# Weight splits, combinations and the norm's root in the first chunks of two MLP stages

## The chip, the cores and the metric

The kernel runs on one core of a Trainium2 chip. The metric is device time in microseconds (us) of the whole program, as the median of several runs. The core has engines that each work through a queue of their own in order: TensorE (PE in the profile, with its weight loads as PEld), VectorE (DVE), ScalarE (ACT), GpSimd (POOL) and SyncE (SP), which here issues the transfers. An instruction that waits holds up all that stands behind it in its queue.

## The reference

The program computes a trunk of two layers for 768 tokens (a sequence of 512 and one of 256) of width 1024. Layer 0 mixes tokens by windowed attention, layer 1 by a short gated convolution. Behind each mixer come the MLP and a gated embedding. The MLP, where the change lies, is the two lines in the middle:

```python
def rms_norm(x, g):
    y = x * lax.rsqrt(jnp.mean(x * x, axis=-1, keepdims=True) + EPS)
    return y * g
...
for i in range(DEPTH):
    h = rms_norm(x, norm_mix[i])
    x = x + mixer(h)
    h = rms_norm(x, norm_mlp[i])
    x = x + jnp.square(jax.nn.relu(h @ mlp_w_up[i])) @ mlp_w_down[i]
    gate = jax.nn.sigmoid(rms_norm(x, norm_ple[i]) @ ple_w_gate[i])
    x = x + (p[i] @ ple_w_proj[i]) * gate
return rms_norm(x, final_norm)
```

All is in float32. `mlp_w_up` is 1024 x 4096, `mlp_w_down` 4096 x 1024.

## The kernel before, in words

**Float32 from three products.** Every operand of a matmul is split into a rounded high part (a copy by ACT) and a low part (the difference, by DVE), and a product is high x high + high x low + low x high. So each weight tile costs a copy on ACT (`high`, line 409) and a subtraction on DVE (`low`, line 420) before PE can use it. `zhi` and `zlo`, `whi` and `wlo`, `vhi` and `vlo` are such pairs; the tag `z` has one buffer, `w` two.

**Tiling of the MLP.** The 4096 hidden features are cut into 16 chunks of 256 (`u` = 0 to 15), two chunks make a group `g`, and after each group come two `down` jobs (`h` = 0, 1), which add the group's part to `x`. Tokens lie along the free axis in two halves of 384. A *plain* chunk (`up_plain`) multiplies its two 128-feature weight tiles with both token halves straight: four results `p1`, `p2` (two banks each), 24 matmuls for each bank. The other chunks (`up`) and all `down` jobs use a scheme with seven products for a 2 x 2 block instead of eight (`product7`), which needs sums of weight blocks (`sums32`, `sums14`) and *combinations* of activation blocks: `norm.combine(m)` makes, for each of four pairs of blocks of `x`, two scaled copies `q` on ACT, four half-width steps on DVE (`t13`, `t42`), two high copies on ACT and two low parts on DVE. `PLAIN = 3, 2` says that chunks 0, 1, 2 are plain in the first MLP (`mlp0`) and chunks 0, 1 in the second (`mlp1`): the time they take on PE is used to make the combinations. In `mlp1` two of the four combinations are made ahead of it (`early = 2`), in `mlp0` none.

**The norm.** The gain is multiplied into `x` when its blocks are split (`Norm7.block`), and the factor 1/root is applied to the chunk's result (`rectified`, line 863). For it the squares of all blocks are added up in `acc`; `acc_parts` splits the sum (`ah`, `al`), `sum_squares` adds over partitions by four matmuls with ones (`ss`), and `rstd_steps` gives three steps: `logs` (an ACT table load, `v` on DVE, `ln` twice and `y` = exp on ACT), `newton` (a square on ACT, `v` on DVE) and `result` (`rstd` on DVE).

**Order.** Inside `mlp` the order on PE, ACT and DVE is the order of the program's text (`manual_schedule`); what stands ahead of it, the mixer's output projection with its adds, squares and block splits, is ordered by a scheduler and may be mixed with the first instructions of `mlp`. The list `pend` holds the steps that make a finished chunk's activations ready for `down`; `late()` takes one of them, `weave` takes one step from each of several lists in turn.

`up_plain` issues its matmuls in four parts, n = 0 to 3, and after each part the work of the other engines. For chunk 0 the parts are: blocks 0 to 5 into `p1`, the same into `p2`, blocks 6 and 7 into `p1`, and into `p2`. For later chunks they are one bank each: `p1` and `p2` of the second token half, then `p1` and `p2` of the first. Behind part 0 stand the next chunk's fetch (`make`) and the split of its `second` weight tile (`whi`, `wlo`), woven with a combination; behind part 1 another combination and `pend`; behind part 2 the split of the next chunk's `direct` tile (`zhi`, `zlo`), which waits until PE has read the old one for the last time; behind part 3, in chunk 0, the root with a third combination. Then `rectified` empties the banks and `squared` follows. The next chunk's first matmul reads `zhi`, its third `zlo`.

In the listing, lines 170 to 261 are the norm, 879 to 950 `up_plain`, 952 to 1005 `up`, 1079 to 1092 the list of jobs. In the trace `mlp0` starts at 310.4 us with chunk 0, 1 at 327.8, 2 at 352.8; `mlp1` at 1144.0 with chunk 0, 1 at 1161.5, 2 at 1178.3.

Of the kernel before, what the change touches and what calls it, by code (L numbers as in the profile page):

```python
# [18 lines left out]
P = 128  # L19
D = 1024  # L20
KB = D // P
# [14 lines left out]
NG = FF // (FG * P)  # L36

H = T // 2
# [3 lines left out]
EXP_LN = "natural_log_exp_and_others"  # L42
# [5 lines left out]
def trunk_kernel(ctx: ExitStack, tc: tile.TileContext, a: dict, out: bass.AP):  # L48
# [56 lines left out]
    def bank(tag, name):  # L105
        return psum.tile([P, 512], F32, tag=tag, name=name, bufs=BANKS[tag])
# [9 lines left out]
    def both(name="mm", tag=None):  # L116

        return [t[:, :H] for t in fresh(name, 2, tag)]
# [52 lines left out]
    class Norm:  # L171
# [30 lines left out]

        aside = temp

        def acc_parts(self):
            ah, al = self.aside("ah", F32R), self.aside("al", F32R)
            self.last = split(ah, al, self.acc)
            return ah, al

        def sum_squares(self, psum, also=None, parts=None, tag=None):  # L210

# [22 lines left out]
        def rstd_steps(self, psum, ss=None):  # L234
            n = self.n
            if ss is None:
                ss = self.sum_squares(psum)
            v, ln, y = (self.aside(name) for name in ("v", "ln", "y"))

            def logs():  # L240
                with tc.issue_after(self.last):
                    act.preload_act_table_set(EXP_LN)
                for t, o, e in ss:
                    dve.tensor_scalar(v[:, o:e], t, 1.0 / D, EPS, ALU.mult, ALU.add)  # L244
                for t, o, e in ss:
                    act.activation(ln[:, o:e], t, AF.Ln, scale=1.0 / D, bias=eps[:])  # L246
                act.activation(y, ln, AF.Exp, scale=-0.5)  # L247


            def newton():  # L250
                act.activation(ln, y, AF.Square)  # L251
                dve.scalar_tensor_tensor(v, ln, -0.5, v, ALU.mult, ALU.mult)  # L252

            def result():
                if self.rplace is None:
                    self.r = stat.tile([P, n], F32, tag="rstd", name=f"rstd_{self.name}")[:]
                else:
                    self.r = slot(self.rplace, f"rstd_{self.name}", F32)[:, :n]
                dve.scalar_tensor_tensor(self.r, v, 1.5, y, ALU.add, ALU.mult)  # L259

            return [logs, newton, result]
# [184 lines left out]
    def mixer_attention():  # L446
# [36 lines left out]
                yield ps[:, :n], o, o + n  # L483
                o += n

        def step(i, w, part, tag, vector):

            l, m = i // KB, i % KB
            if tag == "L":
                t = ap.tile([P, T], F32, tag="L", name="pjs", bufs=BL)  # L490
            else:
                t = big("pjs")
            for ps, o, e in products(terms_of(w, part, col=m % 4 * P)):
                if vector:
                    dve.tensor_copy(t[:, o:e], ps)
                else:
                    act.activation(t[:, o:e], ps, AF.Copy)
            nc.sync.dma_start(pj[l][m], t[:])

        with tc.manual_schedule(engines=order):  # L500
# [31 lines left out]
            w0 = blocks(hi[:], 2), blocks(lo[:], 2)  # L532
            w1 = weight(None, 2, raw=w1)
            for i in range(KB):
                step(i, (w0, w1)[i // 4], part0, "L", i % 2)
# [13 lines left out]
        with s1:  # L549
# [208 lines left out]

            def projected(q):
                w = weight(a["proj"][1, q], 2)  # L760
                for i in range(4):
                    step(KB + 4 * q + i, w, part1, "t", False)

            part1 = [], []

# [87 lines left out]
    def mlp(l, norm, nxt, w, places, early):  # L853
# [11 lines left out]
        def squared(t):  # L865
            act.activation(t[:], t[:], AF.Square)  # L866
# [24 lines left out]
        def late(n=1):  # L891

            for _ in range(n):
                if pend:
                    pend.pop(0)()

        def up_plain(u, w, make, then):

            nonlocal r

            ps = [both(f"p{i + 1}", {0: "AA", 1: "BC"}.get(u, "AA")[i]) for i in range(2)]
            y1 = y2 = None

            def rects(*which):
                for i, o in which:
                    rectified((y1, y2)[i], ps[i][o], H * o, H * o + H, ALU.max)


            order = [(0, (0, 6), (0, 1)), (1, (0, 6), (0, 1)), (0, (6, 8), (0, 1)), (1, (6, 8), (0, 1))]
            if u > 0:  # L910
                order = [(i, (0, 8), (o,)) for o in (1, 0) for i in range(2)]
            for n, (i, ks, sides) in enumerate(order):
                for k in range(*ks):
                    m, h = PAIRED[k] % (KB // 2), PAIRED[k] // (KB // 2)
                    c = slice(P * m, P * m + P)
                    hi, lo = w.w[f"w{i + 1}{h + 1}"]
                    for j, (wt, part) in enumerate(((hi, 0), (hi, 1), (lo, 0))):
                        for o in sides:
                            pe.matmul(
                                ps[i][o],  # L920
                                lhsT=wt[:, c],
                                rhs=xs[f"x{h + 1}{1 + o}"][m][part],
                                start=k == 0 and j == 0,
                                stop=k == KB - 1 and j == 2,
                            )
                if n == 0:
                    v = make()
                    split2 = [lambda: v.split("second")] if v.plain else []
                    todo1 = norm.combine(todo.pop(0)) if todo else []
                    rest, pend[:] = pend[:4], pend[4:]  # L930
                    weave(rest, todo1, split2)
                elif n == 1:
                    if r is None:
                        parts = norm.acc_parts()
                    sums = [] if v.plain else [v.sums32, v.sums14, lambda: v.split("direct")]
                    weave(norm.combine(todo.pop(0)) if todo else [], sums, pend)
                    pend.clear()
                elif n == 2:
                    v.split("direct" if v.plain else "s32")
                    if u > 0:  # L940
                        y1, y2 = big("y1"), big("y2")
                        rects((0, 1), (1, 1))
                else:
                    if r is None:
                        steps = norm.rstd_steps(psum, norm.sum_squares(psum, parts=parts, tag="C"))
                        weave(steps, norm.combine(todo.pop(0)) if len(todo) > 1 else [])
                        r = norm.r
                        y1, y2 = big("y1"), big("y2")
                        rects((0, 1), (1, 1))
                    rects((0, 0))  # L950
                    squared(y1)
                    rects((1, 0))
                    pend.extend(acts_of(u, y1, y2, y2))
            return v

        def up(u, w, make, then):

            w.low("s32")
            w.split("s14")
            late()  # L960
            v = make()
            seven = isinstance(v, Weights7)
            a = bank("A", "a")[:, :H]
            product7(a, w, "w11", xs, True)
            late()
            c = bank("C", "c")[:, :H]
            act.activation(c, a, AF.Copy)  # L967
            late()
            w.split("w22")
            late()  # L970
            b = bank("B", "b")[:, :H]
            product7(b, w, "s3", xs, True)
            p = big("p")[:, :H]
            act.activation(p, b, AF.Copy)
# [101 lines left out]
                        add(m, ps[i])  # L1076
                        nxt.block(m, x(m))

        jobs = [(up_plain, 0), (up_plain, 1)]
        for g in range(NG - 1):  # L1080
            jobs += [(up if 2 * g + 2 >= PLAIN[l] else up_plain, 2 * g + 2), (down, g, 0), (down, g, 1), (up, 2 * g + 3)]
# [159 lines left out]

    n1 = Norm7(2, "mlp0", xs0, act0[7:11], act0[11])
    w0, behind = first_chunk(0, n1, 0)
    w = [weight(a["w_o0"][2], 4), weight(a["w_o2"], 2)]
    for i, m in enumerate(PAIRED):
        if i == 4:
            w[0] = weight(a["w_o0"][3], 4)
        ps = both()
        if m < KB // 2:
            group2(ps, terms_of(w[0], [p[4:] for p in aos], col=m % 2 * P))  # L1250
        else:
            group2(ps, terms_of(w[1], [p[6:] for p in aos], col=(m - 4) * P))
        add(m, ps, xa[m])
        n1.block(m, x(m))
        behind(i)
# [96 lines left out]
```

## Time and profile before

| | us |
|---|---|
| median of 3 runs | 1716.2 |
| lowest and highest | 1715.09, 1717.12 |
| the profiled execution | 1715.87 |
| its span, first to last instruction | 1714.1 |
| PE busy | 1672.0 |
| DVE busy | 1339.6 |
| ACT busy | 855.7 |

Rows of a timeline read: start in us, busy us, engine, line of the kernel, operation, output<-input, partitions x elements, how many in a row; in brackets the idle time just ahead and what ended it. Starts of instructions that follow each other closely lie nearer than their busy times, since the engines overlap the end of one with the start of the next. Rows of waits read: engine, what waited, for whom, us in total, how often, the longest. Rows of windows read: stretch, its length, then busy time of PE, PEld, DVE, ACT and POOL with the number of instructions, the clock granted to PE as a share of full, the share of DMA engines busy, and GB/s.

### The profile page before, as it was taken

The numbers are of one execution on the slowest core, as the hardware profiler recorded it, in microseconds if no ns is written. First come the engines' busy times: TensorE is split into PE (matmuls) and PEld (weight loads), VectorE is DVE, ScalarE is ACT, GpSimd is POOL, SyncE is SP. The second block draws the span as 40 slices with busy tenths as digits, with TensorE's granted clock in tenths as the row PEclk, the third lists the DMA queues.
The fourth block names the chain that finished last, engine by engine and source line by source line (L and its number), as shares of the span: only waits on it lengthen the run. The fifth ranks groups of instructions, "written<-read, shape, count | busy, mean of one in ns | idle before, by whom it ended". The sixth has DMA issues, their size and how long they took to land. (4 is left out here: it accounts for less than half of the span.)

```text
span 1714.1 us, 24208 instructions
## 1 busy us (share of the span) xinstructions
PE 1672.0 (98%) x9554; PEld 1616.8 (94%) x9554; DVE 1339.6 (78%) x2198; ACT 855.7 (50%) x1363; POOL 2.0 (0%) x30
## 2 busy tenths in 40 slices
PE   8999999979999999999999999999999999999996
PEld 7887878979999999999999999999999999999986
DVE  7587788878999999977764444667989999999676
ACT  6467756645455455545541111445455555545454
POOL 0000000000000000000000000000000000000000
PEclk9999999989999999999999999999999999999998
DMA  8653331112221222122312121211221222222222
GB/s 263 189 146 110 114 109 62 45 50 74 65 84 62 75 74 74 62 84 93 108 62 62 62 62 62 76 60 49 74 73 64 74 75 74 65 71 86 74 89 96
DMA packets 47554, 143.80 MB, mean 84 GB/s; under 512 B 6048, under 2 KB 10656, under 8 KB 47440
## 3 DMA queue, kind: packets, MB, share of 16 engines
q1 hardware_dynamic: 44880, 139.10, 25.8%
q10 hardware_dynamic: 2560, 3.15, 0.7%
q8 instruction: 75, 1.23, 0.3%
q14 instruction: 39, 0.32, 0.1%
HBM read 122.31 MB, written 10.48 MB: 77 GB/s over the span
## 5 line engine op out<-in xcount | busy, mean ns | idle before, releaser
L83 ACT ACTIVATE whi<-wraw 128x1024 fp32r<-128x1024 f32 (+2 forms) x74 | 76.6, 1035 | 183.9 <-PE b L129 53.2
L409 ACT ACTIVATE whi<-sum 128x1024 fp32r<-128x1024 f32 x55 | 57.9, 1053 | 146.6 <-PE a L441 146.6
L866 ACT ACTIVATE y<-y 128x768 f32<-128x768 f32 x64 | 53.4, 838 | 140.5 <-DVE y L863 140.5
L84 DVE TENSOR_TENSOR wlo<-wraw,whi 128x1024 fp32r<-128x1024 f32 (+2 forms) x74 | 88.2, 1191 | 11.7 <-ACT whi L83 11.4
L441 PE MATMUL a<-act,whi 128*128 128x384 f32 x448 | 96.7, 337 | 0.0
L441 PE MATMUL a<-t,zhi 128*128 128x384 f32 x440 | 90.7, 337 | 1.8 <-ACT c L967 1.8
L441 PE MATMUL b<-t,zhi 128*128 128x384 f32 x440 | 90.5, 337 | 0.9 <-DVE y L863 0.9
L441 PE MATMUL a<-t,whi 128*128 128x384 f32 x440 | 90.5, 337 | 0.0
L1023 DVE TENSOR_TENSOR x<-x,a 128x384 f32<-128x384 f32 x112 | 60.8, 553 | 35.1 <-PE a L441 34.8
L441 PE MATMUL a<-xs,whi 128*128 128x384 f32 x432 | 84.5, 337 | 0.0
L138 PE MATMUL mm<-xs_mix,whi 128*128 128x512 f32 (+1 forms) x320 | 83.3, 342 | 0.0
L441 PEld LDWEIGHTS a<-t,zhi 128*128 128x128 f32 x440 | 77.9, 188 | 2.1 <-ACT c L967 2.1
L441 PEld LDWEIGHTS a<-act,whi 128*128 128x128 f32 x448 | 79.8, 188 | 0.0
L441 PEld LDWEIGHTS b<-t,zhi 128*128 128x128 f32 x440 | 77.7, 188 | 1.2 <-issue 1.2
L441 PEld LDWEIGHTS a<-t,whi 128*128 128x128 f32 x440 | 77.8, 188 | 0.0
L441 PEld LDWEIGHTS a<-xs,whi 128*128 128x128 f32 x432 | 76.3, 188 | 0.0
L420 DVE TENSOR_TENSOR wlo<-wraw,whi 128x1024 fp32r<-128x1024 f32 x60 | 73.0, 1217 | 1.9 <-ACT whi L409 1.9
L420 DVE TENSOR_TENSOR wlo<-sum,whi 128x1024 fp32r<-128x1024 f32 x55 | 67.2, 1222 | 9.2 <-ACT whi L409 9.2
L409 ACT ACTIVATE whi<-wraw 128x1024 fp32r<-128x1024 f32 x60 | 63.2, 1054 | 17.4 <-issue 10.3
L420 DVE TENSOR_TENSOR zlo<-sum,zhi 128x1024 fp32r<-128x1024 f32 x55 | 66.9, 1217 | 1.9 <-ACT zhi L409 1.9
L409 ACT ACTIVATE zhi<-sum 128x1024 fp32r<-128x1024 f32 x55 | 58.3, 1060 | 19.9 <-DVE sum L385 16.1
L330 ACT ACTIVATE t<-y 128x768 fp32r<-128x768 f32 x56 | 47.0, 841 | 40.6 <-DVE y L321 27.9
(279 smaller groups left out, 4647.9 us busy)
## 6 DMA issues: line engine op xcount, KB each, us to landing
wraw<-in_up SPq DMA_DIRECT2D x64, 512.0 KB, 3.5
wraw<-in_down SPq DMA_DIRECT2D x64, 512.0 KB, 3.5
wraw<-in_w_in SPq DMA_DIRECT2D x24, 512.0 KB, 3.4
wraw<-in_gate SPq DMA_DIRECT2D x16, 512.0 KB, 3.5
pj<-pjs SPq DMA_DIRECT2D x16, 384.0 KB, 2.9
wraw<-in_w_q SPq DMA_DIRECT2D x8, 512.0 KB, 4.9
wraw<-in_w_out SPq DMA_DIRECT2D x8, 512.0 KB, 3.4
x_in<-in_x SPq DMA_DIRECT2D x8, 384.0 KB, 7.2
```

Source lines behind the costliest of these rows:

```text
L83: first = act.activation(hi, src, AF.Copy)
L84: dve.tensor_tensor(lo, src, hi.bitcast(F32), ALU.subtract)
L138: pe.matmul(ps[:, o:e], lhsT=w, rhs=x[:, o:e], start=i == 0 and j == 0, stop=i == n - 1 and j == 2,)
L330: act.activation(t[0][:], (self.q1, self.q2)[i][:], AF.Copy)
L409: act.activation(hi[:], src, AF.Copy)
L420: dve.tensor_tensor(lo[:], src, hi[:].bitcast(F32), ALU.subtract)
L441: pe.matmul(ps, lhsT=a, rhs=b, start=start and i == 0, stop=i == len(terms) - 1, skip_group_check=True)
L866: act.activation(t[:], t[:], AF.Square)
L1023: dve.tensor_tensor(t[:, o : o + H], t[:, o : o + H], f, op)
```

## The change

The table load leaves `logs` for a method of its own, which loads once:

```diff
+        ready = False
+        def table(self):
+            if not self.ready:
+                with tc.issue_after(self.last):
+                    act.preload_act_table_set(EXP_LN)
+            self.ready = True
...
             def logs():
-                with tc.issue_after(self.last):
-                    act.preload_act_table_set(EXP_LN)
+                self.table()
```

In `up_plain`, chunk 0 (`not known`) splits the sum of squares and loads the table behind part 0, ahead of the combination; adds over partitions behind part 0 where `early` is set (`mlp1`) and behind part 1 otherwise; and takes the root behind part 1, with one combination between `logs` and `newton`. The split of the next chunk's direct tile stays behind part 2 in chunk 0, and moves ahead of part 1's combination in later chunks. Only two combinations are left in chunk 0 of `mlp0`.

```diff
+            known = r is not None
...
                 if n == 0:
                     v = make()
                     split2 = [lambda: v.split("second")] if v.plain else []
-                    todo1 = norm.combine(todo.pop(0)) if todo else []
                     rest, pend[:] = pend[:4], pend[4:]
-                    weave(rest, todo1, split2)
+                    if not known:
+                        parts = norm.acc_parts()
+                        norm.table()
+                    weave(rest, norm.combine(todo.pop(0)) if todo else [], split2)
+                    if not known and early:
+                        ss = norm.sum_squares(psum, parts=parts, tag="C")
                 elif n == 1:
-                    if r is None:
-                        parts = norm.acc_parts()
+                    if not known and not early:
+                        ss = norm.sum_squares(psum, parts=parts, tag="C")
+                    steps = [] if known else norm.rstd_steps(psum, ss)
+                    for step in steps[:1]:
+                        step()
+                    if known and v.plain:
+                        v.split("direct")
                     sums = [] if v.plain else [v.sums32, v.sums14, lambda: v.split("direct")]
                     weave(norm.combine(todo.pop(0)) if todo else [], sums, pend)
                     pend.clear()
+                    for step in steps[1:]:
+                        step()
+                    r = norm.r
                 elif n == 2:
-                    v.split("direct" if v.plain else "s32")
-                    if u > 0:
+                    if not v.plain:
+                        v.split("s32")
+                    elif not known:
+                        v.split("direct")
+                    if known:
                         y1, y2 = big("y1"), big("y2")
                         rects((0, 1), (1, 1))
                 else:
-                    if r is None:
-                        steps = norm.rstd_steps(psum, norm.sum_squares(psum, parts=parts, tag="C"))
-                        weave(steps, norm.combine(todo.pop(0)) if len(todo) > 1 else [])
-                        r = norm.r
+                    if not known:
                         y1, y2 = big("y1"), big("y2")
-                        rects((0, 1), (1, 1))
+                        rects((0, 1))
                     rects((0, 0))
                     squared(y1)
+                    if not known:
+                        rects((1, 1))
                     rects((1, 0))
```

In `up`, the first chunk behind the plain ones of `mlp1` (`first`) takes its results `c` and `b` from bank tag A instead of C and B, and takes its first three `late` steps behind the copy into `c`:

```diff
+            first = u == PLAIN[l] <= 2
...
-            late()
+            if not first:
+                late()
...
-            late()
-            c = bank("C", "c")[:, :H]
+            if not first:
+                late()
+            c = bank("A" if first else "C", "c")[:, :H]
             act.activation(c, a, AF.Copy)
-            late()
+            late(3 if first else 1)
...
-            b = bank("B", "b")[:, :H]
+            b = bank("A" if first else "B", "b")[:, :H]
```

The places of the activations in `mlp0` are taken in another order; the second combination gets 14, 0, 1 and 2 instead of 14, 16, 17 and 18 (16 to 19 hold the attention's output before, 0 to 6 a copy of `x`):

```diff
-    xs0 = [*range(32, 42), *range(8, 15), *range(16, 20), *range(7)]
+    xs0 = [*range(32, 42), *range(8, 15), *range(7), *range(16, 20)]
```

The rest (how `step`, the list of jobs and the weights of the last output projection are written) leaves the instructions and their order as they were. The number of matmuls, copies and subtractions is the same; PE's queue differs only in the place of the eight `ss` matmuls.

More of the change, by code (lines that the diff above doesn't have):

```diff
@@ L484, in products, with step @@
                 o += n
-        def step(i, w, part, tag, vector):
-            l, m = i // KB, i % KB
+        def step(l, m, w, part, tag, vector):
             if tag == "L":
@@ L534, in mixer_attention @@
             for i in range(KB):
-                step(i, (w0, w1)[i // 4], part0, "L", i % 2)
+                step(0, i, (w0, w1)[i // 4], part0, "L", i % 2)
                 norm.block(i, xin(i))
@@ L760, in projected @@
                 w = weight(a["proj"][1, q], 2)
-                for i in range(4):
-                    step(KB + 4 * q + i, w, part1, "t", False)
+                for m in range(4 * q, 4 * q + 4):
+                    step(1, m, w, part1, "t", False)
             part1 = [], []
@@ L1077, in last_down @@
                         nxt.block(m, x(m))
-        jobs = [(up_plain, 0), (up_plain, 1)]
+        ups = [(up if u >= PLAIN[l] else up_plain, u) for u in range(2 * NG)]
+        jobs = ups[:2]
         for g in range(NG - 1):
-            jobs += [(up if 2 * g + 2 >= PLAIN[l] else up_plain, 2 * g + 2), (down, g, 0), (down, g, 1), (up, 2 * g + 3)]
+            jobs += [ups[2 * g + 2], (down, g, 0), (down, g, 1), ups[2 * g + 3]]
         with tc.manual_schedule(engines={ET.Activation, ET.PE, ET.DVE}):
@@ L1243, in trunk_kernel @@
     w0, behind = first_chunk(0, n1, 0)
-    w = [weight(a["w_o0"][2], 4), weight(a["w_o2"], 2)]
+    w = [weight(a["w_o0"][2], 4)] * 2
+    w2 = weight(a["w_o2"], 2)
     for i, m in enumerate(PAIRED):
         if i == 4:
-            w[0] = weight(a["w_o0"][3], 4)
+            w += [weight(a["w_o0"][3], 4)] * 2
         ps = both()
         if m < KB // 2:
-            group2(ps, terms_of(w[0], [p[4:] for p in aos], col=m % 2 * P))
+            group2(ps, terms_of(w[m], [p[4:] for p in aos], col=m % 2 * P))
         else:
-            group2(ps, terms_of(w[1], [p[6:] for p in aos], col=(m - 4) * P))
+            group2(ps, terms_of(w2, [p[6:] for p in aos], col=(m - 4) * P))
         add(m, ps, xa[m])
```

2 lines of the change are left out of this document (1 added, 1 removed).

## The prediction

> **What bounds the kernel now.** PE does. I read the page's first part, then PE's waits over the stretch that holds both MLP stages.
>
> ```profile
> PE 1672.0 (98%) x9554; PEld 1616.8 (94%) x9554; DVE 1339.6 (78%) x2198; ACT 855.7 (50%) x1363; POOL 2.0 (0%) x30
> ```
>
> ```profile
> PE p L919 <- ACT zhi L409: 8.0, 1, 8.0
> PE a L441 <- ACT c L967: 1.8, 1, 1.8
> PE p L919 <- DVE zlo L420: 1.4, 1, 1.4
> PE b L441 <- DVE y L863: 0.9, 1, 0.9
> ```
>
> The number of matmuls stays, so only PE's idle time, and its clock, can change. The change can reach these four waits: 8.0 and 1.4 us in `mlp0`, where chunk 2 waits for its direct weights, and 0.9 and 1.8 us in `mlp1`, in the first seven-product chunk. Next, PE's timeline over chunks 1 and 2 of `mlp0`, and the same time in windows.
>
> ```profile
> 327.84 0.51 PE L919 MATMUL p<-x,zhi 128*128 128x384 f32 x2
> ...
> 352.79 1.01 PE L919 MATMUL p<-x,zhi 128*128 128x384 f32 x2 [8.01 <-ACT zhi L409]
> ...
> 361.15 0.51 PE L919 MATMUL p<-x,whi 128*128 128x384 f32 x2
> ```
>
> ```profile
> 327.80:344.80 17.00, 16.98 (x98) 16.66 (x96) 10.08 (x17) 11.91 (x16) 0.00 (x0) 1.00 0.11 32
> 344.80:352.80 8.00, 0.01 (x1) 0.01 (x1) 7.71 (x12) 4.79 (x7) 0.00 (x0) 0.79 0.21 66
> 352.80:356.00 3.20, 1.83 (x5) 1.32 (x6) 3.20 (x6) 0.00 (x0) 0.00 (x0) 0.50 0.00 0
> 356.00:359.50 3.50, 3.50 (x13) 3.50 (x11) 1.73 (x5) 2.72 (x4) 0.00 (x0) 0.50 0.41 150
> ```
>
> A matmul takes 17.00 / 98 = 0.173 us at full clock, so chunk 2's first bank of 24 should take 4.2 us. It took 361.15 - 352.79 = 8.4: 1.4 of the excess is the wait for `zlo`, 2.8 is the clock, which falls to 0.50 during the idle time and stays there until 359.5. The stall costs **8.0 + 4.2 = 12.2 us**, more than the waits show.
>
> Chunk 1, at 327.84, starts without a wait: its `zhi` and `zlo` are ready. Whether that holds after the change is the question.
>
> **The change part by part.** *What is removed.* From the order in which the changed program's instructions stand: chunk 2's direct split now stands ahead of chunk 1's second combination and waits only for PE's third part of chunk 1. A copy of 1.04 and a subtraction of 1.22 behind that fit into PE's fourth part (4.2 us), so the 12.2 us go. In `mlp1`, `b` and `c` no longer wait for banks that chunk 1's `rectified` must empty, nor `c`'s copy for older steps: 0.9 + 1.8 = 2.7 us go. In all, 14.9.
>
> *What is moved in front of chunk 1's direct split.* On ACT, chunk 0 now has `ah`, table load, two `q`, `whi`, two high copies, `ln` twice, `y`, two `q`, two high copies, the Newton square, and only then `zhi` of chunk 1. Before, the table load, `ln`, `y` and the square stood behind it. All durations are in the rows of before, ACT's first, then DVE's:
>
> ```profile
> 320.00 0.84 ACT L83 ACTIVATE ah<-acc_mlp 128x768 fp32r<-128x768 f32 x1
> 320.74 0.92 ACT L303 ACTIVATE q<-x,vec 128x768 f32<-128x768 f32 x1
> 321.56 0.93 ACT L304 ACTIVATE q<-x,vec 128x768 f32<-128x768 f32 x1
> ...
> 325.12 1.04 ACT L409 ACTIVATE zhi<-wraw 128x1024 fp32r<-128x1024 f32 x1
> ...
> 329.82 1.28 ACT L242 ACT_TABLE_LOAD   x1
> 331.12 1.05 ACT L246 ACTIVATE ln<-ss,eps 128x384 f32<-128x384 f32 x2
> 332.20 0.85 ACT L247 ACTIVATE y<-ln 128x768 f32<-128x768 f32 x1
> ```
>
> ```profile
> 314.87 0.95 DVE L196 TENSOR_TENSOR acc_mlp<-acc_mlp,sq 128x768 f32<-128x768 f32 x1
> 315.74 2.35 DVE L420 TENSOR_TENSOR wlo<-wraw,whi 128x1024 fp32r<-128x1024 f32 x2
> ...
> 323.72 0.56 DVE L326 SCALAR_TENSOR_TENSOR q<-q 128x384 f32<-128x384 f32 x1
> 324.19 2.01 DVE L336 TENSOR_TENSOR t<-q,t 128x768 fp32r<-128x768 f32 x2
> 326.20 1.22 DVE L420 TENSOR_TENSOR zlo<-wraw,zhi 128x1024 fp32r<-128x1024 f32 x1
> 327.68 1.02 DVE L244 TENSOR_SCALAR v<-ss 128x384 f32<-128x384 f32 x2 [0.26 <-PE ss L226]
> ...
> 334.95 0.96 DVE L259 SCALAR_TENSOR_TENSOR rstd_mlp<-v,y 128x768 f32<-128x768 f32 x1
> ```
>
> The chain in `mlp0`, step by step. The last addition to `acc` ended at 314.87 + 0.95 = 315.8; one low split of weights (half of 2.35) now stands ahead of it: 317.0. ACT: `ah` (0.74 to the next start), table load 1.28, `q` 0.82, `q` 0.93: 320.8; the copy `whi` 1.04: 321.8. DVE stands at that `wlo`: 1.2, so 323.0; two half-width steps of 0.56: 324.1; two low parts 2.0: 326.1; only behind them, in DVE's queue, is the first `v`, 0.5: 326.6, though the `ss` matmuls, now ahead of chunk 0's parts 2 and 3, are long done. ACT, whose `ln` started behind `v` in the row above too: `ln` twice 1.05, `y` 0.74, two `q` 0.82 + 0.93: 330.1. DVE: three half steps of 0.56: 331.8. ACT: a high copy and the Newton square, 0.75 apart each: 333.3; **`zhi` 1.04: 334.3**. PE has finished chunk 0 at 327.84 as before, so it **waits 6.5 us**. DVE from 331.8: two low parts 2.0, two steps of 0.96 to `rstd`, **`zlo` 1.22: 336.9**, 2.6 behind `zhi`, where the two matmuls before it take 0.35 at full clock: about 2 more. A stall of this size was measured above: wait for `zlo` and half clock together cost 4.2, which I take again (bounds 2.0, no clock loss, and 5.5, as long at half clock once more). **Chunk 1 pays 6.5 + 4.2 = 10.7 us.** The wait holds up on ACT and DVE all that is queued behind `zhi` and `zlo`: chunk 0's `rectified`, `squared` and chunk 1's combination, none of which PE waits for within chunk 1, as its banks are others.
>
> *One combination more in chunk 1.* It moves there from chunk 0 and stands between chunk 2's direct split and chunk 1's `rectified`. How near that comes to PE is seen at the first `down`, which needs the banks of chunk 2:
>
> ```profile
> 355.04 1.94 DVE L863 SCALAR_TENSOR_TENSOR y<-p,rstd_mlp 128x384 f32<-128x384 f32 x4
> ...
> 370.67 1.23 DVE L420 TENSOR_TENSOR zlo<-sum,zhi 128x1024 fp32r<-128x1024 f32 x1 [1.90 <-ACT zhi L409]
> 371.81 1.48 DVE L863 SCALAR_TENSOR_TENSOR y<-p,rstd_mlp 128x384 f32<-128x384 f32 x3
> ```
>
> From the first of these rows to the second bank emptied (371.81 + 1.0) are 17.8 us, some 15 to 16 without the wait in brackets and ACT's delays. Behind the end of PE's third part of chunk 1 there now come `zhi` and `zlo` (2.3), then four half steps, and four low parts for `pend` and the combination (5.7), then those 15: 23.0, while PE needs its fourth part and chunk 2, 4.2 + 96 x 0.174 = 20.9. I take 1.6 us of waiting there, with bounds 0 and 2.5.
>
> *`mlp1`.* Here chunk 1 started without a wait, and chunk 2 is no plain one, so there is nothing to gain ahead of it.
>
> ```profile
> 1144.00 1.02 DVE L806 TENSOR_TENSOR x<-x,mm 128x384 f32<-128x384 f32 x2 [4.26 <-PE mm L129]
> ...
> 1147.51 0.95 DVE L196 TENSOR_TENSOR acc_mlp<-acc_mlp,sq 128x768 f32<-128x768 f32 x1
> ```
>
> ```profile
> 1161.46 0.51 PE L919 MATMUL p<-x,zhi 128*128 128x384 f32 x2
> ```
>
> The last adds end at 1145.0; block split, low part and addition to `acc` follow with nothing between (0.9 + 1.0 + 1.0): 1147.9. The same chain from `ah` to `zhi`'s end is 334.3 - 317.0 = 17.3: 1165.2. PE asks at 1161.46: **3.7 us, and about 2.0 for `zlo`**. For the clock I have rows on both sides: the 0.9 and 1.8 of `mlp1` show no cost, the 8.0 cost 2.8. With 5.7 us idle, broken only by two matmuls, I take 1.5.
>
> [...]
>
> *At no cost.* The table is loaded as often as before. The swapped places only free the second combination of a wait that it did not show. SP's queue has the same transfers in the same order; one weight fetch goes out some 9 us later, when chunk 1's `zlo` frees its buffer, but its data are wanted only behind chunk 2. If that cover went, ACT's high copies would be late at the first `down`, where the 1.6 stand already. POOL does nothing here. The `ss` matmuls, 0.17 each, only change places.
>
> **Sum**: -12.2 + 10.7 + 1.6 = +0.1 in `mlp0`; -2.7 + 3.7 + 2.0 + 1.5 = +4.5 in `mlp1`; +4.6 in all. Against the profiled execution's 1715.87 that is 1720.5; the median of the runs shown lies 0.3 above it: **1720.8 us**.
>
> **The rivals.**
>
> *Hardly a change.* The new stalls come, but the clock in `mlp1` stays at 1.00 and DVE catches up before the first `down`: 4.6 - 1.5 - 1.6 = +1.5, 1717.7. For it: the 0.9 and 1.8 left the clock alone. Against it: DVE has no idle time between chunk 1's zlo and those banks in which to catch up.
>
> *Faster, as the stall at chunk 2 goes and none replaces it.* The time would be 1715.87 - 14.9 + 0.3 = 1701.3. It needs chunk 1's `zhi` by 327.84, a chain of 10.8 us from `ah` where I count 17.3. The point that decides is the place of `zhi` behind `y`, two `q` and the Newton square on ACT. Only if ACT or DVE left the order of their queues could it be met, and the rows above start in that order.
>
> *Clearly slower.* The half clock outlasts the restart by 3.5 us more in both stages, 1.75 each, and the bank wait is 2.5: 4.6 + 3.5 + 0.9 = +9.0, 1725.2. [...]
>
> **How the numbers follow.** My forecast has 0.57, its own range 1718.5 to 1723.5 (clock loss in `mlp1` 0 to 2.8, bank wait 0 to 2.5). Hardly a change has 0.22, faster 0.07, clearly slower 0.14. The range 1716.0 to 1725.0 leaves out the faster case and a half of the slower one. 0.2%, about what a measurement of this kernel tells from no change, is 3.4 us: same means 1712.8 to 1719.6. To same go 0.22 and a tenth of my forecast's 0.57: faster 0.07, same 0.28, slower 0.65.
>
> **What would show it.** In the profile after: at the head of chunk 1 in `mlp0` an idle of about 6.5 us ended by ACT `zhi`, then about 1.4 to 2 by DVE `zlo`, and none at chunk 2; in `mlp1` the same pair with 3.7 and 2.0 (less where the clock is low); the waits of `b` for `y` and of `a` for `c` gone; a wait of 1 to 2 us for a bank at the first `down` of `mlp0`; the granted clock at 0.50 in both heads. I am wrong if chunk 1 of `mlp0` starts within 2 us of chunk 0's end, or if chunk 2 still waits for its `zhi`.

## The result, and the profile after

| | before | after |
|---|---|---|
| median of 7 runs | 1716.20 | 1720.83 |
| lowest and highest | 1714.29, 1718.31 | 1718.84, 1721.81 |
| span of the profiled execution | 1714.1 | 1719.2 |
| PE busy | 1672.0 | 1673.8 |

The ratio is 1.0025, with a 95% interval from 1.0013 to 1.0036: slower by 4.6 us.

PE's waits after, over both MLP stages (what waited, for whom, us in total, times, longest):

```profile
PE p L927 <- ACT zhi L417: 10.6, 2, 6.6
PE p L927 <- DVE zlo L428: 2.6, 2, 1.3
PE a L449 <- DVE y L870: 1.6, 1, 1.6
PE b L449 <- DVE zlo L428: 1.3, 6, 0.2
```

The 8.0 us for `zhi` at chunk 2, the 1.8 for `c` and the 0.9 for `y` are gone. In their place `zhi` is waited for twice, 6.6 us in `mlp0` and 4.0 in `mlp1`, `zlo` twice, 1.3 each, and the first `down` waits 1.6 us for a bank; the last row, six waits of 0.2 us in later groups, hardly counts. PE's timeline after says where:

```profile
335.05 1.01 PE L927 MATMUL p<-x,zhi 128*128 128x384 f32 x2 [6.59 <-ACT zhi L417]
337.37 0.69 PE L927 MATMUL p<-x,zlo 128*128 128x384 f32 x1 [1.30 <-DVE zlo L428]
...
343.76 0.51 PE L927 MATMUL p<-x,whi 128*128 128x384 f32 x2
...
356.31 0.51 PE L927 MATMUL p<-x,zhi 128*128 128x384 f32 x2
...
1166.11 1.01 PE L927 MATMUL p<-x,zhi 128*128 128x384 f32 x2 [3.98 <-ACT zhi L417]
1168.42 0.69 PE L927 MATMUL p<-x,zlo 128*128 128x384 f32 x1 [1.30 <-DVE zlo L428]
...
1174.07 0.51 PE L927 MATMUL p<-x,whi 128*128 128x384 f32 x2
```

The stall of `mlp0` now stands at the head of chunk 1 (335.05); chunk 2 (356.31) starts without one. The 24 matmuls of chunk 1's first bank take 343.76 - 335.05 = 8.7 us where 4.2 would do, so the stall costs 6.6 + 4.5 = 11.1 us in `mlp0`; in `mlp1` it costs 4.0 + (1174.07 - 1166.11 - 4.2) = 7.8.

The net of each stage is read best from the same matmul in both traces: the first of chunk 0 in `mlp0`, one of chunk 3, one of the mixer's last ahead of `mlp1`, and one of the first seven-product chunk of `mlp1`. PE's timeline before, then after:

```profile
310.37 0.34 PE L919 MATMUL p<-xs,zhi 128*128 128x384 f32 x1
...
424.11 1.57 PE L441 MATMUL c<-xs,whi 128*128 128x384 f32 x8
...
1142.93 0.87 PE L129 MATMUL mm<-ys,whi 128*128 128x384 f32 x4
...
1192.03 1.57 PE L441 MATMUL d<-t,vhi 128*128 128x384 f32 x8
```

```profile
310.83 0.34 PE L927 MATMUL p<-xs,zhi 128*128 128x384 f32 x1
...
425.32 1.55 PE L449 MATMUL c<-xs,whi 128*128 128x384 f32 x8
...
1143.43 0.87 PE L129 MATMUL mm<-ys,whi 128*128 128x384 f32 x4
...
1197.18 1.57 PE L449 MATMUL d<-t,vhi 128*128 128x384 f32 x8
```

After is later by 0.46, 1.21, 0.50 and 5.15 us. So 0.46 us were there before `mlp0` began, its head costs 0.75 us net, 0.71 are gained on the way to `mlp1`, and the head of `mlp1` costs 4.65. 0.46 + 0.75 - 0.71 + 4.65 = 5.15, as between the spans: nearly all of the change's cost lies in the second stage.

The gain on the way is no delay made up, for PE waits for nothing there in either trace. 0.6 of the 0.71 us come from one run of matmuls, the products `b` in layer 1's mixer. Before, then after; these rows give the shortest, middle and longest duration in ns, then the first and the last start:

```profile
L129 PE MATMUL b<-xs_mix,wlo x128: 332/337/341, 892.6 to 1076.7; 128*128 128x384 f32 x128
L129 PE MATMUL b<-xs_mix,wlo x128: 332/337/343, 893.7 to 1077.2; 128*128 128x384 f32 x128
```

That is 184.1 us before and 183.5 after. Of the runs below, the three that start from the kernel before have 184.0 or 184.1 there, and the seven that start from the changed kernel 183.4 or 183.5, whatever their stalls are. Some part of the change that these seven share shortens this stretch by 0.6 us; which part it is stays open.

Why `zhi` is late is in ACT's timeline after, from the split of the sum of squares on:

```profile
317.40 0.85 ACT L83 ACTIVATE ah<-acc_mlp 128x768 fp32r<-128x768 f32 x1 [1.26 <-DVE acc_mlp L196]
318.26 1.28 ACT L216 ACT_TABLE_LOAD   x1
319.56 0.94 ACT L311 ACTIVATE q<-x,vec 128x768 f32<-128x768 f32 x1
...
327.03 1.05 ACT L254 ACTIVATE ln<-ss,eps 128x384 f32<-128x384 f32 x2 [1.49 <-DVE v L252]
...
333.96 1.04 ACT L417 ACTIVATE zhi<-wraw 128x1024 fp32r<-128x1024 f32 x1
```

In `mlp1` the same queue:

```profile
1148.45 0.85 ACT L83 ACTIVATE ah<-acc_mlp 128x768 fp32r<-128x768 f32 x1 [1.22 <-DVE acc_mlp L196]
...
1152.28 1.04 ACT L417 ACTIVATE whi<-wraw 128x1024 fp32r<-128x1024 f32 x1
...
1165.02 1.04 ACT L417 ACTIVATE zhi<-wraw 128x1024 fp32r<-128x1024 f32 x1
```

From `ah`'s start to `zhi`'s end are 17.6 us in both. Two brackets matter below: `ah` itself waited 1.2 to 1.3 us for the last sum of the mixer's output, and `ln` 1.49 us for DVE.

### The profile page after: what moved, and what is told of

Read it like the earlier page. It is cut to its first block, busy times and chain, and to the rows that moved or that the text cites. A ratio compares the mean times of both kernels' runs of the same rounds, so it can differ in the third digit from the quotient of the medians.

```text
span 1719.2 us, 24213 instructions
## 1 busy us (share of the span) xinstructions
PE 1673.8 (97%) x9554; PEld 1617.6 (94%) x9554; DVE 1339.4 (78%) x2198; ACT 855.8 (50%) x1363; POOL 2.0 (0%) x30
## 3 DMA queue, kind: packets, MB, share of 16 engines
q10 hardware_dynamic: 2560, 3.15, 0.7%
## 5 line engine op out<-in xcount | busy, mean ns | idle before, releaser
L83 ACT ACTIVATE whi<-wraw 128x1024 fp32r<-128x1024 f32 (+2 forms) x74 | 76.5, 1034 | 184.1 <-PE b L129 53.0
```

What stands on the lines that cost most here:

```text
L83: first = act.activation(hi, src, AF.Copy)
```

## The experiments

Two ways to read the same waits were set against each other. **S** is the bookkeeping of the prediction: each stall belongs to the place of one split or bank, so each part of the change has its price and the prices add up. **B**, a backlog: ACT and DVE come into the head of a stage with a chain of work that PE is faster than; the place of a split decides where PE meets the rest of this chain, and its length decides how long PE waits. Each run was timed beside the kernel before on the same chip, and the ratios below are to that. Waits are PE's in the first chunks of each stage, in us.

| run | median | before | ratio, 95% interval | `mlp0` | `mlp1` |
|---|---|---|---|---|---|
| after | 1720.83 | 1716.20 | 1.0025 [1.0013, 1.0036] | 6.6 + 1.3 + 1.6 | 4.0 + 1.3 |
| split_only | 1715.81 | 1716.62 | 0.9992 [0.9983, 1.0002] | 6.6 + 1.1 | 0.9 + 1.8 |
| banks_only | 1715.67 | 1716.62 | 0.9997 [0.9989, 1.0006] | 8.0 + 1.4 | 1.8 + 0.8 + 0.4 |
| root_only | 1719.50 | 1716.62 | 1.0017 [1.0008, 1.0026] | 6.6 + 1.3 + 1.5 | 4.0 + 1.7 |
| acc_behind | 1714.84 | 1716.62 | 0.9990 [0.9981, 0.9998] | 6.6 + 1.3 + 1.6 | 0.2 + 0.7 |
| root_behind | 1715.58 | 1716.75 | 0.9993 [0.9984, 1.0002] | 2.5 + 0.6 + 1.0 + 3.6 | 0.6 + 1.7 + 0.8 + 0.4 |
| table_late | 1717.65 | 1716.75 | 1.0004 [0.9995, 1.0012] | 5.2 + 1.3 + 1.6 | 2.6 + 1.3 + 0.2 |
| one_less | 1711.87 | 1716.75 | 0.9963 [0.9949, 0.9976] | 2.4 + 1.8 | 0.9 + 1.8 |
| acc_both | 1712.04 | 1716.05 | 0.9972 [0.9961, 0.9984] | 4.2 + 1.3 + 1.6 | 0.2 + 0.7 |
| spread | 1709.74 | 1716.75 | 0.9958 [0.9945, 0.9972] | 1.6 + 0.6 + 3.0 | 0.2 + 0.7 |
| spread_old | 1710.06 | 1716.05 | 0.9960 [0.9947, 0.9972] | 1.6 + 0.6 + 2.7 + 1.5 | 0.2 + 0.7 |

**split_only**: the split's move alone.

```diff
 # before, up_plain, n == 1
+                    if u > 0 and v.plain:
+                        v.split("direct")
                     sums = [] if v.plain else [v.sums32, v.sums14, lambda: v.split("direct")]
 # n == 2
-                    v.split("direct" if v.plain else "s32")
+                    if not v.plain:
+                        v.split("s32")
+                    elif u == 0:
+                        v.split("direct")
```

> The kernel before with one edit: chunk 1 of mlp0 splits chunk 2's direct weights ahead of pend's last steps. Theory S (the prediction's bookkeeping): the place of this split was the stall, so the 8.0 us wait for zhi, the 1.4 for zlo and the 2.8 of half clock go: -12.2, 1704.0 us. Theory B (backlog): ACT and DVE come out of chunk 0 with a queue of work, and the split gains only what it jumps over in the rows of before, ACT's two high copies at 350.23 (1.5 us): a zhi wait of 6.5 us, a zlo wait of 1 to 1.5, the clock still at half: -1.5, 1714.7 us.

ACT's timeline of this run, then PE's:

```profile
349.59 0.84 ACT L330 ACTIVATE t<-q 128x768 fp32r<-128x768 f32 x1 [3.15 <-DVE q L326]
350.34 1.04 ACT L409 ACTIVATE zhi<-wraw 128x1024 fp32r<-128x1024 f32 x1
351.29 1.56 ACT L330 ACTIVATE t<-y 128x768 fp32r<-128x768 f32 x2
```

```profile
351.43 1.01 PE L919 MATMUL p<-x,zhi 128*128 128x384 f32 x2 [6.55 <-ACT zhi L409]
353.55 0.69 PE L919 MATMUL p<-x,zlo 128*128 128x384 f32 x1 [1.11 <-DVE zlo L420]
```

`zhi` now stands ahead of the two high copies that it stood behind, and that is its whole gain: PE waits 6.55 in place of 8.0. The combination of part 0 is still ahead of it, and that one waits 3.15 for DVE. The time is 1.1 us above B's and 12 above S's; the ratio's interval reaches 1, so the gain itself is not clear of the noise.

**banks_only**: in `up` of the kernel before, the `first` lines of the change and nothing else.

```diff
...
-            c = bank("C", "c")[:, :H]
+            c = bank("A" if first else "C", "c")[:, :H]
             act.activation(c, a, AF.Copy)
-            late()
+            late(3 if first else 1)
...
-            b = bank("B", "b")[:, :H]
+            b = bank("A" if first else "B", "b")[:, :H]
```

> The kernel before with one edit: the first seven-product chunk of mlp1 takes c and b from bank tag A and its late steps behind the copy into c. Theory S: the waits of 0.9 (b for DVE y) and 1.8 (a for ACT c) go: -2.7, 1713.5 us. Theory B: ACT and DVE are behind PE there whatever the banks are, so waits of about the same sum (2 to 3.5 us) show up a few products later under other names: -0.5 to +0.5, 1715.7 to 1716.7 us.

Its waits in `mlp1`:

```profile
PE a L441 <- ACT c L970: 1.8, 1, 1.8
PE a L441 <- DVE y L993: 0.8, 1, 0.8
PE b L441 <- DVE zlo L420: 0.4, 1, 0.4
```

3.0 us as before (0.9 + 1.8 + 0.3); the bank wait of `b` is gone and one of `a` has come, for a later `y`. The time, 1715.67, is B's too; S's 1713.5 would be a ratio of 0.998, below the interval.

**root_only**: the changed kernel with these two parts taken out, so the root's move and the combination that leaves chunk 0 remain.

```diff
-                    if known and v.plain:
-                        v.split("direct")
...
-                    if not v.plain:
-                        v.split("s32")
-                    elif not known:
-                        v.split("direct")
+                    v.split("direct" if v.plain else "s32")
...
-            first = u == PLAIN[l] <= 2
+            first = False
```

> The changed kernel with the split of chunk 2's direct weights put back behind part 2 of chunk 1, and c and b on their old banks: what is left of the change is the root's move (and the combination that goes from chunk 0 to chunk 1). Theory S: the new waits of chunk 1 (6.6 + 4.5 in mlp0, 4.0 + 3.8 in mlp1) stand beside the old stall of 12.2 at chunk 2 and the 2.7 of mlp1: 1720.8 + 12.2 + 2.7 - 1.6 = 1734.1 us. Theory B: the wait at chunk 1 gives ACT and DVE the time that they lacked, so at chunk 2 there is only what one more combination ahead of the split costs, 1 to 3.5 us of waiting, and no bank wait in mlp1: 1720 to 1724 us.

PE's waits in `mlp0`:

```profile
PE p L927 <- ACT zhi L417: 6.6, 1, 6.6
PE p L927 <- DVE zlo L428: 2.8, 2, 1.5
```

Chunk 2 has no wait for `zhi` although its split stands behind a whole combination again, only 1.5 for `zlo`; and no bank is waited for in `mlp1`. What the wait at chunk 1 takes from PE it gives to ACT and DVE. The split's new place buys nothing here either: 1.5 at chunk 2 without it, 1.6 at the first `down` with it. The time, 1719.50, is 0.5 us below B's range and 14.6 below S's.

**acc_behind**: the root stays where the change put it, but in `mlp1` the split of the sum of squares goes behind part 0's weave, as it was before.

```diff
-                    if not known:
+                    if not known and not early:
                         parts = norm.acc_parts()
                         norm.table()
                     weave(rest, norm.combine(todo.pop(0)) if todo else [], split2)
+                    if not known and early:
+                        parts = norm.acc_parts()
+                        norm.table()
```

> The changed kernel with, in mlp1 alone, the split of the sum of squares (ah, al) and the table load put back behind part 0's combination and weight split. Theory A: ah waits for the mixer's last sum, and on ACT and DVE the combination, whi and wlo wait behind it for nothing; before, they ran ahead of it. From ah at 1149.8 as before, the rest of the chain (al, ss, v, ln, y, q, q, t, t, square, zhi) is 10 us long and ends ahead of PE's 1161.5: the waits of 4.0 and 1.3 and the half clock go from mlp1, 7.8 us in all, and PE may wait 0.5 to 1.5 for ah and al at the ss products: about -6.6, 1714.2 us. Rival: the cost is the root ahead of zhi itself; then a zhi wait of 2 to 4 us stays in mlp1: -0 to -3, 1718 to 1721 us.

ACT's timeline of this run in `mlp1`:

```profile
1144.62 1.06 ACT L417 ACTIVATE whi<-wraw 128x1024 fp32r<-128x1024 f32 x1 [5.58 <-issue]
1145.59 0.83 ACT L338 ACTIVATE t<-q 128x768 fp32r<-128x768 f32 x1
...
1149.77 0.85 ACT L338 ACTIVATE t<-q 128x768 fp32r<-128x768 f32 x1 [1.79 <-DVE q L334]
1150.52 0.83 ACT L83 ACTIVATE ah<-acc_mlp 128x768 fp32r<-128x768 f32 x1
...
1161.40 1.06 ACT L417 ACTIVATE zhi<-wraw 128x1024 fp32r<-128x1024 f32 x1 [0.69 <-PE p L927]
```

`whi` and the combination run while the mixer's last sums come in. `ah` starts 2.1 us later than after's 1148.45, yet `zhi` starts 3.6 earlier than its 1165.02, and waits for PE instead of PE for it. The ratio falls from 1.0025 to 0.9990, some 6 us; expected by A was -6.6. The root still stands ahead of `zhi`, and all that PE waits for in `mlp1` is 0.9 us at the `ss` matmuls, so the root's place alone is not what cost 7.8 us there. What cost was work placed behind a wait for the last sum that it does not need, and the table load, which moves along in this run: by table_late below up to 1.4 of the 3.6 us are the load's. The bank waits of before do not come back, although chunk 1 no longer waits; spread_old below shows that this is not the new banks' doing.

**root_behind**: the sum split early, as in the changed kernel, but the root behind the direct split.

```diff
-                    steps = [] if known else norm.rstd_steps(psum, ss)
-                    for step in steps[:1]:
-                        step()
...
 # n == 2, behind v.split("direct")
+                    steps = [] if known else norm.rstd_steps(psum, ss)
+                    for step in steps:
+                        step()
+                    r = norm.r
```

> The changed kernel with the whole root (v, ln, y, square, rstd) put behind the direct split in chunk 0 of both stages, part 2, where before it stood behind part 3. Theory S (each stall belongs to the place of one split): the waits of chunk 1 go and nothing takes their place: 6.6 + 4.5 in mlp0 and 4.0 + 3.8 in mlp1, 1720.8 - 18.9 = 1702 us. Theory B (backlog): the root is not gone, only later, so in mlp0 the 9.5 us of waiting (6.6 + 1.3 + 1.6) stay about as they are, spread over chunk 1, chunk 2 and the first down in pieces too short for the clock to fall, which gains some 3 us; in mlp1 the waits of chunk 1 go (7.8) and the 2.7 to 3.5 of before's first seven-product chunk come back, though its banks and late steps are the new ones: -7 to -9, 1712 to 1714 us.

In `mlp0` 9.5 us of waits became 7.7 in four places; in `mlp1` 2.5 us came back at the first seven-product chunk, though it has the new banks and late steps. The time is 1.6 to 3.6 us above B's, where the clock was expected to hold: it still fell twice in `mlp0`, to a mean of 0.64 from 331.1 to 335.5 us and of 0.71 from 372.2 to 378.0. S is off by 13.6.

**table_late**: the load of the table back in `logs`.

```diff
                         parts = norm.acc_parts()
-                        norm.table()
```

> The changed kernel with the table load back in logs, behind the combination of part 0. In the rows of after the load (1.28) stands right behind ah, the q copies behind it, and DVE waits 1.29 for the first q; ACT idles 1.49 ahead of ln, waiting for v. Theory B: without the load ahead of it the whole chain is 1.28 earlier, and the load itself lies in the idle time ahead of ln: both zhi waits shrink by 1.3 (6.6 to 5.3, 4.0 to 2.7), -2.6 or, with the clock, up to -4: 1717 to 1718.3 us. Rival: the load costs its 1.28 in the chain wherever it stands: 1720.8 us, waits as after.

ACT's timeline of this run, around the load:

```profile
324.08 0.85 ACT L338 ACTIVATE t<-q 128x768 fp32r<-128x768 f32 x1 [1.69 <-DVE q L334]
324.95 1.28 ACT L216 ACT_TABLE_LOAD   x1
326.42 1.05 ACT L254 ACTIVATE ln<-ss,eps 128x384 f32<-128x384 f32 x2 [0.19 <-DVE v L252]
```

The load fills the idle time ahead of `ln`, of which 0.19 is left of 1.49. Both waits for `zhi` shrink by 1.4 (6.6 to 5.2, 4.0 to 2.6). So its early place cost 1.4 us in each head; its own 1.28 us cost nothing a little later. The time, 1717.65, lies in B's range.

**one_less**: the kernel before with one combination's work left out; its results are taken from the first combination's.

```diff
 # before, up_plain, n == 3
-                        weave(steps, norm.combine(todo.pop(0)) if len(todo) > 1 else [])
+                        weave(steps)
+                        if len(todo) > 1:
+                            m = todo.pop(0)
+                            for k in ("t1", "t2", "t3", "t4"):
+                                norm.xs[k][m] = norm.xs[k][0]
```

> The kernel before without the work of one combination: the third of mlp0, which stood with the root behind part 3 of chunk 0, is left out (two scaled copies, four half steps, two high copies, two low parts), and its results are taken from the first one's; PE does the same matmuls, and the split of chunk 2's direct weights stays where it was. Theory B: the wait of 8.0 at chunk 2 is a queue of ACT and DVE work, so it shrinks by what the combination took there, 3.3 us on ACT or 4.2 on DVE and up to 5.5 where one waited for the other: to 2.5 to 4.7 us, and with a shorter half clock 1716.6 - 4 to - 8 = 1708.5 to 1712.5 us. Theory S: the place of the split decides, the wait stays within 1 us of 8.0, 1716 us.

With the split where it was, the wait for `zhi` goes from 8.0 to 2.4: 5.6, slightly more than the bound of 5.5 for a combination in which each engine waits for the other. The place of the split is the same and the wait is not: its length comes from the work in the queue. The time, 1711.87, lies in B's range; S's was 1716.

**acc_both**: acc_behind in both stages.

```diff
-                    if not known:
-                        parts = norm.acc_parts()
-                        norm.table()
                     weave(rest, norm.combine(todo.pop(0)) if todo else [], split2)
+                    if not known:
+                        parts = norm.acc_parts()
+                        norm.table()
```

> The changed kernel with the split of the sum of squares and the table load behind part 0's combination and weight split in both stages (acc_behind had it in mlp1 alone, 1714.8 us). Theory B: in mlp0 too the combination and whi ran into ah's wait for the last sum. With ah at 320.0 as in the rows of before, then table 1.28, ln, y, two q, two high copies and the square, with the short waits for DVE's half steps, zhi ends at 331 to 333 where PE asks at 328.4: a zhi wait of 2.5 to 4.5 us in place of 6.6, the bank wait at the first down still 1.6: -2 to -5 against acc_behind, 1710 to 1713 us. Rival: ah, 2.6 us later, brings all of the root that much later, the wait stays 6.6: 1714.8 us.

The wait in `mlp0` falls from 6.6 to 4.2 and the time is 1712.04, both within what B gave. It does not vanish as in `mlp1`. ACT's timeline of this run in `mlp0` shows why:

```profile
323.21 0.85 ACT L338 ACTIVATE t<-q 128x768 fp32r<-128x768 f32 x1 [3.92 <-DVE q L334]
323.96 0.83 ACT L83 ACTIVATE ah<-acc_mlp 128x768 fp32r<-128x768 f32 x1
...
335.04 1.04 ACT L417 ACTIVATE zhi<-wraw 128x1024 fp32r<-128x1024 f32 x1
```

The combination ahead of `ah` itself waits 3.92 us for DVE, so `ah` starts only 8.0 us before PE asks for `zhi` (336.14 - 4.17 = 331.97), where acc_behind had 13.1 in `mlp1` (1150.52 to 1163.64).

**spread**: the orders that helped, together.

```diff
 # n == 0, behind the weave
+                    if not known:
+                        parts = norm.acc_parts()
+                    if not known and early:
+                        norm.table()
...
 # n == 1
-                    steps = [] if known else norm.rstd_steps(psum, ss)
+                    steps = norm.rstd_steps(psum, ss) if not known and early else []
...
 # n == 2, around v.split("direct")
+                    if not known and not early:
+                        steps = norm.rstd_steps(psum, ss)
+                        steps[0]()
...
+                    if not known and not early:
+                        for step in steps[1:]:
+                            step()
+                        r = norm.r
```

> The changed kernel with three orders altered: in both stages the split of the sum of squares stands behind part 0's combination and weight split (table load with it in mlp1, back in logs in mlp0), and in mlp0 the root goes behind part 2, its logs ahead of the direct split and its Newton step behind it. From acc_behind's 1714.8 us, which has the mlp1 part of this. Theory B: in mlp0 the queue is 3 to 5 us shorter, since the combination no longer waits behind ah and the load finds an idle ACT; what is left shows as a zhi wait of 1 to 2, a zlo wait of 1 and a bank wait of 3 to 3.5 at the first down, too short each for the clock to fall for long: 6.6 + 4.5 + 1.6 = 12.7 becomes 5 to 7, 1707 to 1709.5 us. Rival: the queue in mlp0 is not shortened, 9.5 us of waits stay and only the clock's 3 us come back: 1712 us.

Its two longest waits in both stages:

```profile
PE a L449 <- DVE y L870: 3.0, 1, 3.0
PE p L927 <- ACT zhi L417: 1.6, 1, 1.6
```

1709.74, 0.2 above the range of B, and 7.0 us faster than the kernel before. What is left in `mlp0` is the 3.0 us for a bank at the first `down`.

**spread_old**: spread without the two parts that root_only took out (the same edit as there).

> The kernel of spread (1709.7 us) with two parts of the change taken out: chunk 2's direct weights are split behind part 2 of chunk 1, as before, and c and b of mlp1's first seven-product chunk are on their old banks, with the old late steps. Theory S (the prediction's bookkeeping): the 12.2 us at chunk 2 and the 2.7 in mlp1 come back, 1724.6 us. Theory B: the split only decides where the rest of the queue shows: the bank wait of 3.0 at the first down becomes a zhi wait of 2.5 to 3.5 and a zlo wait of 1 to 2 at chunk 2, with a shorter or no half clock, and mlp1 has no bank wait: 1709.7 + 0 to + 4, so 1709.5 to 1714 us.

1710.06 at a ratio of 0.9960 against 0.9958: no difference. The 3.0 us at the bank became 2.7 + 1.5 at chunk 2. In none of the three settings in which they were tried (split_only and banks_only, root_only, spread_old) are those two parts of the change worth anything clear of the noise.

## Why the prediction was right, and where not

**The chain in front of chunk 1's `zhi`** was right: 17.3 us predicted, 17.6 measured; waits of 6.5 and 3.7, measured 6.6 and 4.0. In `mlp0`, `zlo` and the half clock were put at 4.2 and measured 4.5; in `mlp1` at 2.0 + 1.5 and measured 3.8. What was not seen is what this chain is made of. The prediction took it as the root's price; acc_behind shows that in `mlp1` the wait goes although the root stays: it comes from the combination and `whi` that now stand behind `ah`'s wait, and from the load. table_late shows that the load's early place is 1.4 us of the wait in each head; the prediction counted the load in the chain but did not name it as avoidable.

**"What is removed"**, 14.9 us in all, is the step that failed, though its numbers appear. The stall of 12.2 us did go, but not because the split "now stands ahead of chunk 1's second combination and waits only for PE's third part": split_only, with the split ahead of all that stood behind part 1, keeps 6.6 + 1.1 of it, and root_only, without it, has no `zhi` wait at chunk 2. The chunk is asked for some 11 us later, and the chain is done by then. The same holds for the 2.7 us in `mlp1`: banks_only keeps 3.0. The removal and the new stall were in the main one effect, a late chain that PE meets at chunk 1 instead of chunk 2, counted as a gain and a loss; so the sum came out although the gain was put down to the wrong cause. Two things were not taken apart in any run: the combination that leaves chunk 0 of `mlp0`, and the later place of `rects((1, 1))`, stand in every run that starts from the changed kernel.

**The bank wait at the first `down`** was put at 1.6 and is 1.6. It too is the chain's rest: it grows where work is put behind `zhi` (spread 3.0, root_behind 3.6), goes to chunk 2 where the split does (spread_old, 2.7 + 1.5), and stays 1.6 where only the wait for `zhi` shrinks (table_late, acc_both).

**The sum**: `mlp0` +0.1 predicted, +0.75 measured; `mlp1` +4.5 and +4.65. By the terms measured above, `mlp0` should have lost 11.1 + 1.6 - 12.2 = 0.5 and `mlp1` 7.8 - 2.7 = 5.1, so each is accounted for to within 0.5. Two things lay outside the sum and about cancel: 0.46 us from ahead of `mlp0`, whose cause was not looked into, and the 0.6 to 0.7 us gained ahead of `mlp1`. That the forecast 1720.8 came within 0.1 us of the measured median is luck: the clock alone moved the same stall by 1.1 us between two runs, as the last section shows. The 1.5 us for the clock in `mlp1` rested on the kernel before, where the waits of 0.9 and 1.8 us left the clock alone (1.00 from 1178.27 to 1192.00 us); in split_only the same two waits were followed by 3.42 us at 0.50 (1185.72 to 1189.14).

**The rivals.** "Hardly a change" needed the clock in `mlp1` to stay at 1.00 and no bank wait at the first `down`; neither held, as the forecast had it (6.83 us at 0.50, and 1.6 us of waiting). "Faster" was said to hang on `zhi` behind `y`, two `q` and the square. Spread puts the square behind `zhi` and runs the first combination and `whi` ahead of `ah`, and is 7.0 us faster than the kernel before, though not at 1701.3, since a part of the chain is left. "Clearly slower" needed the half clock to outlast the restart in both stages; it ended within the first bank of chunk 1 in both, at 342.75 and 1172.2 us.

## What to carry to other kernels

When a stall moves, ask whether its work has become less: add up the waits over the whole stage, for a part that only changes where the fast engine meets a late chain gained nothing here, however large the wait that it removed. An instruction that waits for the last result of the stage before is best put behind work that does not need that result, as in acc_behind (some 6 us). A fixed cost such as a table load goes where its engine is already waiting for another: in table_late that took 1.4 us off the wait for `zhi` in each head.

## What the runs showed of the hardware

The same stall did not cost the same clock. After and root_only have the same code up to there and the same 6.6 us of waiting at chunk 1; their windows are (wait, then restart; behind the busy times of five engines comes the granted clock):

```profile
328.46:335.05 6.59, 0.00 (x1) 0.00 (x0) 4.80 (x7) 5.51 (x7) 0.00 (x0) 0.81 0.00 0
335.05:343.76 8.71, 7.40 (x24) 6.90 (x25) 6.49 (x11) 5.49 (x8) 0.00 (x0) 0.56 0.21 62
```

```profile
325.94:332.54 6.60, 0.01 (x1) 0.00 (x0) 4.80 (x7) 5.53 (x7) 0.00 (x0) 0.88 0.00 0
332.54:341.24 8.70, 7.39 (x31) 6.89 (x32) 6.46 (x11) 5.48 (x8) 0.00 (x0) 0.70 0.20 62
```

In one run the restart had a clock of 0.56 and its first bank took 8.7 us, in the other 0.70, and the same bank was done 7.6 us after its start (the next group of weights starts at 340.11). That is 1.1 us between two runs of the same work.

In windows of 0.05 us over after's two heads the clock reads 1.00 or 0.50, but for the four windows in which it changes. So a mean below 1.00 gives the time at 0.50: in after (1 - 0.81) x 2 x 6.59 + (1 - 0.56) x 2 x 8.71 = 10.2 us, in root_only (1 - 0.88) x 2 x 6.60 + (1 - 0.70) x 2 x 8.70 = 1.6 + 5.2 = 6.8. Windows laid on these stretches in after read 0.50 throughout for 10.24 us in `mlp0` (332.51 to 342.75) and for 6.83 in `mlp1` (1165.37 to 1172.20). In `mlp0` the half clock began 4.0 us into the wait in after and, with 1.6 of the 6.60 us, 5.0 in root_only. In `mlp1` of after it was 4.0 us of waiting, then 1.3, that came with the 6.83 us, while spread's 1.6 + 0.6 at chunk 1 of `mlp0` left the clock at 1.00 (328.85 to 336.00).

A short wait did not always leave the clock alone. In split_only a wait of 1.8 us in the first seven-product chunk of `mlp1` was followed by half clock:

```profile
1182.31:1185.72 3.41, 1.58 (x9) 1.26 (x8) 1.92 (x3) 3.41 (x6) 0.00 (x0) 1.00 0.00 0
1185.72:1189.14 3.42, 3.42 (x13) 3.42 (x12) 3.35 (x7) 1.57 (x4) 0.00 (x0) 0.50 0.02 2
```

PE was busy for 1.58 us of the first stretch, and the clock read 0.50 through the second. The kernel before had the same 1.58 us in the same place (1182.25 to 1185.66) and kept the full clock, 1.00 from 1178.27 to 1192.00. What decides between the two was not shown.
